# Two of four channel groups of a 31-tap depthwise convolution, as products with diagonal matrices on TensorE

## The chip, the cores and the metric

The kernel runs as one program on one core of a Trainium2 chip. The metric is the device time of one execution in microseconds (us); a lower time is better. Engines are named as in the profile: PE is TensorE, DVE is VectorE, ACT is ScalarE, POOL is GpSimd, SP issues most DMAs.

## The reference

Two transformer-like blocks run one after the other on 512 rows of width 1024. The first has a mixer with two branches (a gated convolution and a latent attention) and a feed-forward part; the second has sparse attention, a recurrent branch and a mixture of experts. The change touches only the convolution branch of the first block:

```
def conformer_conv(u, dw_w, dw_b, ln_g, ln_b):
    a, gte = jnp.split(u, 2, axis=-1)
    v = a * jax.nn.sigmoid(gte)
    v = dwconv(v, dw_w, dw_b)          # 31 taps, one filter per channel, 512 channels
    return jax.nn.silu(layer_norm(v, ln_g, ln_b))
```

Beside it, from the same normalised input, the attention branch computes latent rows `cq` and `ckv` (products with `w_in`), an RMS norm of each row, and from these queries, keys and values.

## The kernel before, in words

All of it is in `block1`. Channels lie on partitions, so the 512 channels are four groups of 128. Products are made in three parts with fp32r operands: `split` writes a high part on ACT and the rest on DVE, and `mm3` (lines 85 to 87) issues three matmuls, high by high, low by high, high by low.

The work around the change stands in this order in the code.

1. **Gate stage.** For each group `c`, two products `lin` of 24 matmuls of 512 columns give the gate and the value; ACT takes the sigmoid (line 464) and DVE writes `vpad[:, c]` (line 467), the gated rows with 15 zeros on either side. Between them go steps of `mods`: each loads 1 MB of `w_ada` and issues four fp32 matmuls (line 286).
2. **Latent stage.** Ten products `lat`, six of 288 columns (keys and values) and four of 384 (queries), 24 matmuls each. After each, `rms_rows` squares the row on ACT (line 518), DVE and POOL make the inverse root (lines 123 and 124, `ss`), DVE scales the row (line 520, `cn`). One product later PE transposes `cn` (line 541). Key rows also get a rotation on DVE (lines 508 to 511) and POOL (lines 512 and 513, `krow`). After each product come one or two steps of `mods` and `go(conv, 4)`.
3. **Expansion stage.** Products of the latent rows with `w_ukv` (512 columns, into `dbank`) and `w_uq` (384 columns), again with `go(conv, ...)`, and then the attention proper, whose first PE work is the transposes of line 655.

The convolution itself is the generator `taps`, which `go(conv, n)` advances. Groups 0 to 2 are on DVE: one `scalar_tensor_tensor` per tap (line 486), 93 with the first ones. Group 3 is on POOL: a product (line 479) and a sum (line 481) per tap. The sums `cacc` are first read by `conv_norm` (line 630), inside the attention.

The order of instructions on each engine is not that of the code: a scheduler sets it from its own estimate of times, engine by engine, and each engine then runs its list in order. A pool `psd` holds two PSUM tiles `dbank`; `mods` holds one of them until it ends. The out-projection behind the attention ends in a layer norm of four row tiles `xr` (lines 779 to 786), whose transposed, split rows `hh` and `hl` (lines 163 and 164) feed the feed-forward part.

Of the kernel before, what the change touches and what calls it, by code (L numbers as in the profile page):

```python
# [9 lines left out]
F32 = mybir.dt.float32  # L10
F32R = mybir.dt.float32r
# [3 lines left out]
AF = mybir.ActivationFunctionType  # L15
ALU = mybir.AluOpType
# [4 lines left out]
S = 512  # L21
# [39 lines left out]
class Kernel:  # L61
# [203 lines left out]
    def close(self, *cms):  # L265
        for cm in cms:
            cm.__exit__(None, None, None)
# [70 lines left out]
    def block1(self):  # L338
        tc, nc, io = self.tc, self.nc, self.io
        v, act, pe, pool_e = nc.vector, nc.scalar, nc.tensor, nc.gpsimd  # L340
        op, close = self.open, self.close
# [7 lines left out]
        pC_cm, pC = op("pC", side="left")  # L349
# [3 lines left out]
        pA_cm, pA = op("pA", side="right")  # L353
# [28 lines left out]
        vpad = pV.tile([128, 4, S + 30], F32, name="vpad")  # L382
        cacc = pV.tile([128, 4, S], F32, name="cacc")
# [12 lines left out]
        _, mt = self.mod_turn(md[:, 0:512], pLw)  # L396
# [13 lines left out]
        col = self.col  # L410
# [12 lines left out]
        pM_cm = pM = None  # L423
# [24 lines left out]
        go = lambda gen, n: [None for _ in range(n) if next(gen, 0) == 0]  # L448
# [4 lines left out]
        for c in range(4):  # L453
# [13 lines left out]
            v.tensor_tensor(vpad[:, c, 15:S + 15], psa, sg, op=ALU.mult)  # L467
            go(mods, 1 if c >= 0 else 0)

        def taps():  # L470
            cw = col["conv_dw_w"]
            todo = [[(c, i) for c in range(3) for i in range(31)], [(3, i) for i in range(31)]]
            while todo[0]:
                for eng, lst, n in ((v, todo[0], 3), (pool_e, todo[1], 1)):
                    for _ in range(n):
                        c, i = lst.pop(0)
                        if eng is pool_e and i:
                            w = pC.tile([128, S], F32, name="tap")
                            eng.tensor_scalar(w, vpad[:, c, i:i + S], cw[:, i * 4 + c:i * 4 + c + 1], 1.0,
                                              op0=ALU.mult, op1=ALU.mult)  # L480
                            eng.tensor_tensor(cacc[:, c, :], cacc[:, c, :], w, op=ALU.add)
                        elif i == 0:
                            eng.tensor_scalar(cacc[:, c, :], vpad[:, c, 0:S], cw[:, c:c + 1], col["conv_dw_b"][:, c:c + 1],
                                              op0=ALU.mult, op1=ALU.add)
                        else:
                            eng.scalar_tensor_tensor(cacc[:, c, :], vpad[:, c, i:i + S], cw[:, i * 4 + c:i * 4 + c + 1],  # L486
                                                     cacc[:, c, :], op0=ALU.mult, op1=ALU.add)
                        yield
        conv = taps()


# [10 lines left out]
        def rope(dst, src, t, nh):  # L502

            cs = self.rope[:, t, 0:16].unsqueeze(1).to_broadcast([128, nh, 16])
            sn = self.rope[:, t, 16:32].unsqueeze(1).to_broadcast([128, nh, 16])
            a, b = src[:, :, 0:16], src[:, :, 16:32]
            w = pLw.tile([128, 8, 32], F32, name="ropew")
            v.tensor_tensor(w[:, :nh, 0:16], b, sn, op=ALU.mult)
            v.tensor_tensor(w[:, :nh, 16:32], a, sn, op=ALU.mult)
            v.tensor_tensor(dst[:, :, 0:16], a, cs, op=ALU.mult)  # L510
            v.tensor_tensor(dst[:, :, 16:32], b, cs, op=ALU.mult)
            pool_e.tensor_tensor(dst[:, :, 0:16], dst[:, :, 0:16], w[:, :nh, 0:16], op=ALU.subtract)
            pool_e.tensor_tensor(dst[:, :, 16:32], dst[:, :, 16:32], w[:, :nh, 16:32], op=ALU.add)
# [11 lines left out]
        def lat(t, wts, n):  # L525
            a, b, sl = (hch, hcl, slice(t * 128, (t + 1) * 128)) if t < 2 else (h1h, h1l, slice((t - 2) * 128, (t - 1) * 128))
            ps = self.bank()
            for k in range(8):
                wh, wl = wts[k // 4]
                self.mm3(ps[:, :n], (a[:, k, sl], b[:, k, sl]), (wh[:, k % 4, :], wl[:, k % 4, :]), k == 0, k == 7)  # L530
            return ps

        def latent(ps, t, n, g, hi, lo):
            cn = pLw.tile([128, 384], F32, name="cn")
            rms_rows(cn[:, :n], ps[:, 0:n], n, g)
            return cn, t, n, hi, lo
# [10 lines left out]
        def flush(n=0):  # L547
            while len(pend) > n:
                turn_latent(*pend.pop(0))

        for t in range(6):
            ps = lat(t, wk, 288)
            if t < 2:
                act.activation(krow[:, t, :], ps[:, 256:288], AF.Copy)
            else:
                rope(krow[:, t:t + 1, :], ps[:, 256:288].unsqueeze(1), t - 2, 1)
            pend.append(latent(ps, t, 256, kg, ckh, ckl))
            flush(1)
            go(mods, 1)
            go(conv, 4)  # L560
        wq = [self.wblock(w_in, 4 * h, 4, 1024, 384) for h in range(2)]
        for t in range(NT):
            pend.append(latent(lat(t + 2, wq, 384), t, 384, qg, cqh, cql))
            flush(1)
            go(mods, 2)
            go(conv, 4)
        flush()
        go(mods, 99)
        close(pM_cm, pA_cm)
        pQ_cm, pQ = op("pQ", side="right")  # L570
        k96 = pQ.tile([128, 6, 8, 96], F32, name="k96")
        q96 = pQ.tile([128, NT, 8, 96], F32, name="q96")
# [2 lines left out]
        for t in range(6):  # L575
            pool_e.tensor_scalar(k96[:, t, :, 64:96], krow[:, t:t + 1, :].to_broadcast([128, 8, 32]), 1.0, 1.0,
                                 op0=ALU.mult, op1=ALU.mult)
# [129 lines left out]
        for i in range(len(items)):  # L707
            h, t = items[i]
# [35 lines left out]
        for n in range(2):  # L744
            c = slice(n * 512, (n + 1) * 512)
# [22 lines left out]
        for t in range(NT):  # L768
# [5 lines left out]
            for n in range(2):  # L774
                c = slice(n * 512, (n + 1) * 512)
# [4 lines left out]
            s, b, _ = self.ln_stats([xr[:, 0:512], xr[:, 512:1024]], LN_EPS)  # L780
# [17 lines left out]
        pM_cm, pM = op("pM2", 2, side="right")  # L798
# [71 lines left out]
        hh, hl = self.hh, self.hl  # L870
# [23 lines left out]
        for t in range(NT):  # L894
            sl = slice(t * 128, (t + 1) * 128)
            y = ys[t]
            for k in range(18, 22):
                down(ks, ws, t, k)
            for n in range(2):
                c = slice(n * 512, (n + 1) * 512)  # L900
# [1453 lines left out]
```

## Time and profile before

| | us |
|---|---|
| median of 3 runs | 2093.3 |
| lowest and highest of them | 2086.33 and 2097.59 |
| profiled execution, its own time | 2086.47 |
| its span in the trace | 2084.7 |
| PE busy | 1918.0 (92%) |
| DVE busy | 1175.3 (56%) |
| ACT busy | 661.3 (32%) |
| POOL busy | 555.2 (27%) |

The span is what the trace shows; the profiled execution's own time has 1.8 us around it. Busy shares are means over a program of many stages; the change lies in the first ninth of it, so what it is worth is read from the rows of that part.

### The profile page before, as it was taken

What the parts mean: (1) busy time and instruction counts of PE and PEld (TensorE: products, weight loads), DVE (VectorE), ACT (ScalarE), POOL (GpSimd) and SP (SyncE); (2) the same over time, 40 slices, a digit from 0 to 9 for tenths busy, and PEclk for the clock granted to TensorE, in tenths of its full rate; (3) what the DMA queues carried; (4) which work ended last, traced back from release to release, by engine and by line L of the source; (5) the groups of instructions that cost most, each with busy time, mean ns of one, the idle gap of its engine ahead of it and who ended that gap; (6) DMA issues with size and microseconds to landing.
All of it is one profiled execution on the core that took longest, in us unless ns stands there. A gap on an engine that the chain in (4) does not pass through costs nothing.

```text
span 2084.7 us, 30137 instructions
## 1 busy us (share of the span) xinstructions
PE 1918.0 (92%) x11420; PEld 1461.2 (70%) x11427; DVE 1175.3 (56%) x2137; ACT 661.3 (32%) x1168; POOL 555.2 (27%) x448
## 2 busy tenths in 40 slices
PE   4978898979999998997899999999899999999993
PEld 2657786777777887875677877788676666767662
DVE  4896576588574468565897576667332332222223
ACT  3213466434333325544323245523111111111111
POOL 1279422352012432012002100143122322223222
PEclk8989899989999999999799999999899999999997
DMA  8651102378462223549767631553999999999895
GB/s 284 215 185 60 51 1 78 110 253 296 141 208 97 101 91 115 153 127 236 223 177 177 170 114 62 172 166 133 358 327 360 306 381 329 354 362 336 316 367 173
DMA packets 208751, 425.47 MB, mean 204 GB/s; under 512 B 46694, under 2 KB 140280, under 8 KB 182485
## 3 DMA queue, kind: packets, MB, share of 16 engines
q1 hardware_dynamic: 184914, 366.98, 50.6%
q0 software_dynamic: 15488, 39.41, 7.7%
q10 hardware_dynamic: 8195, 17.06, 2.2%
q8 instruction: 92, 1.51, 0.3%
q14 instruction: 62, 0.51, 0.1%
HBM read 375.37 MB, written 60.08 MB: 209 GB/s over the span
## 4 chain that ended last, share of the span: by engine, by line
PE 70%; DVE 10%; DMA 7%; issue 5%; ACT 3%; POOL 3%; SPq 1%; POOLq 0%; ACTq 0%; DVEq 0%
PE bank L85 10%; PE bank L87 10%; PE bank L86 10%; PE gbank L2146 9%; PE wbank L2201 6%; PE bank L2132 3%; PE bank L2109 2%; PE gbank L2157 2%; PE dbank L85 2%; PE dbank L87 2%; PE dbank L86 2%; DVE cacc L486 1%; DMA ysum_db<-y,idxr 1%; DVE wlo L81 1%; PE wbank L2190 1%
## 5 line engine op out<-in xcount | busy, mean ns | idle before, releaser
L81 DVE TENSOR_TENSOR wlo<-raw,whi 128x1024 fp32r<-128x1024 f32 (+2 forms) x163 | 221.0, 1376 | 111.5 <-ACT whi L80 107.6
L85 PE MATMUL bank<-hh,whi 128*128 128x512 f32 (+3 forms) x720 | 273.2, 383 | 3.5 <-DVE hh L163 3.0
L86 PE MATMUL bank<-hl,whi 128*128 128x512 f32 (+3 forms) x720 | 273.4, 381 | 1.5 <-DVE hl L164 1.5
L87 PE MATMUL bank<-hh,wlo 128*128 128x512 f32 (+3 forms) x720 | 273.1, 382 | 1.0 <-DVE wlo L81 1.0
L80 ACT ACTIVATE whi<-raw 128x1024 fp32r<-128x1024 f32 (+2 forms) x163 | 161.7, 1025 | 241.9 <-PE bank L86 175.9
L2146 PE MATMUL gbank<-wr,xt 128*128 128x256 f32 x928 | 210.5, 385 | 0.9 <-issue 0.3
L2146 PEld LDWEIGHTS gbank<-wr,xt 128*128 128x128 f32 x928 | 175.7, 192 | 24.9 <-ACT xt L2115 1.0
L87 PEld LDWEIGHTS bank<-hh,wlo 128*128 128x128 f32 (+2 forms) x720 | 137.0, 191 | 35.3 <-issue 3.9
L85 PEld LDWEIGHTS bank<-hh,whi 128*128 128x128 f32 (+2 forms) x720 | 137.2, 192 | 32.1 <-DVE hh L163 3.4
L86 PEld LDWEIGHTS bank<-hl,whi 128*128 128x128 f32 (+2 forms) x720 | 137.7, 191 | 29.3 <-DVE hl L164 2.3
L2201 PE MATMUL wbank<-wr,ht 128*128 128x512 f32 (+2 forms) x456 | 138.7, 599 | 6.6 <-ACT ht L2173 5.6
L2162 DVE TENSOR_TENSOR h<-gbank,h 128x256 f32<-128x256 f32 (+1 forms) x40 | 17.0, 426 | 217.0 <-ACT h L2161 217.0
L2183 DVE SCALAR_TENSOR_TENSOR y<-wbank,wt,g2l 128x512 f32<-128x512 f32 (+1 forms) x69 | 51.7, 750 | 129.6 <-PE wbank L2201 110.3
L2201 PEld LDWEIGHTS wbank<-wr,ht 128*128 128x128 f32 (+2 forms) x456 | 51.2, 154 | 73.1 <-issue 62.8
L866 POOL TENSOR_TENSOR hid<-ug,uv 128x512 f32<-128x512 f32 x22 | 36.1, 1643 | 181.3 <-DVE uv L850 181.3
L486 DVE SCALAR_TENSOR_TENSOR cacc<-vpad,cols,cacc 128x512 f32<-128x512 f32 x90 | 83.6, 968 | 0.4
L2161 ACT ACTIVATE h<-gbank 128x256 f32<-128x256 f32 (+1 forms) x40 | 15.2, 381 | 210.8 <-PE gbank L2146 174.8
L2098 POOL DMA_INDIRECT xg<-h_d,idx x40 | 41.1, 1028 | 129.8 <-DVE idx L2093 80.2
L621 POOL TENSOR_TENSOR raw<-raw,g2row 128x2048 f32<-128x2048 f32 x11 | 55.0, 4999 | 73.8 <-DMA raw<-in_w_down_dram 73.5
L2132 PE MATMUL bank<-wr,xt 128*32 128x256 f32 (+1 forms) x896 | 65.9, 381 | 0.7 <-ACT xt L2115 0.2
L1990 POOL DMA_INDIRECT ysum_da<-y,idx x21 | 32.8, 1560 | 118.6 <-DVE y L2183 86.1
L2109 PEld LDWEIGHTS bank<-ident,xg 128*128 128x128 f32 (+1 forms) x392 | 48.8, 195 | 20.3 <-issue 15.3
(692 smaller groups left out, 4263.5 us busy)
## 6 DMA issues: line engine op xcount, KB each, us to landing
wr<-in_exp_gate_dram SPq DMA_DIRECT2D x52, 1024.0 KB
wr<-in_exp_up_dram SPq DMA_DIRECT2D x52, 1024.0 KB
wr<-in_exp_down_dram SPq DMA_DIRECT2D x52, 1024.0 KB
raw<-in_w_in_dram SPq DMA_DIRECT2D x58, 512.0 KB
mraw<-in_w_ada_dram SPq DMA_DIRECT2D x24, 1024.0 KB
mraw<-in_ada_w_dram SPq DMA_DIRECT2D x24, 1024.0 KB
raw<-in_w_up_dram SPq DMA_DIRECT2D x22, 1024.0 KB
raw<-in_w_down_dram SPq DMA_DIRECT2D x11, 1024.0 KB
```

The source lines that it names most:

```text
L80: self.nc.scalar.activation(hi, src, AF.Copy)
L81: self.nc.vector.tensor_tensor(lo, src, hi.bitcast(F32), op=ALU.subtract)
L85: mm(out, a[0], b[0], start=start, stop=False, skip_group_check=True)
L86: mm(out, a[0], b[1], start=False, stop=False, skip_group_check=True)
L87: mm(out, a[1], b[0], start=False, stop=stop, skip_group_check=True)
L486: eng.scalar_tensor_tensor(cacc[:, c, :], vpad[:, c, i:i + S], cw[:, i * 4 + c:i * 4 + c + 1], cacc[:, c, :], op0=ALU.mult, op1=ALU.add)
L621: return lambda raw, k, n: pool_e.tensor_tensor(raw, raw, row.unsqueeze(1).to_broadcast([128, k, n]), op=ALU.mult)
L2109: pe.transpose(ps[:, k * 128:k * 128 + r], x.rearrange("s (p k) -> s k p", k=8)[0:r, 4 * g + k, :], self.ident[0:r, 0:r])
L2132: pe.matmul(ps[to, 0:256], job.xt[:, k, sl], x[:, k * 256:(k + 1) * 256], start=k == 0, stop=k == 7, skip_group_check=True)
L2146: pe.matmul(ps[:, m * 256:(m + 1) * 256], job.xt[:, k, :], w[m][:, k * 256:(k + 1) * 256], start=k == 0, stop=k == 7, skip_group_check=True)
L2183: end = lambda c, ps: v.scalar_tensor_tensor(y[r, c], ps, job.wt[r], g2row[r, c], op0=ALU.mult, op1=ALU.mult)
L2201: pe.matmul(ps[to], job.ht[:, k, sl], x[:, k * D + c.start:k * D + c.stop], start=k == 0, stop=k == 1, skip_group_check=True)
```

## The change

Groups 0 and 1 of the convolution leave DVE. For each of their 62 taps ACT makes two diagonal matrices of 128 x 128, the identity scaled per partition by the high and the low part of that tap's weights; `mm3` then adds diagonal times shifted rows to `cps`, a `dbank` that holds both groups. The rows `vpad` of the two groups and the weights are split once. At the end of a group ACT copies the sum to `cacc` and adds the bias. Group 2 stays on DVE and group 3 on POOL, so `taps` now yields 62 times instead of 124. `go(conv_pe, 6)` and `go(conv_pe, 7)` stand in the latent stage, and `go(conv_pe, 99)` at its end.

```
--- before.py
+++ after.py
@@ -467,25 +467,44 @@
             v.tensor_tensor(vpad[:, c, 15:S + 15], psa, sg, op=ALU.mult)
             go(mods, 1 if c >= 0 else 0)
 
+
+        pD_cm, pD = op("pD", side="right")
+        wc = [pD.tile([128, 62], F32R, name="wc" + x) for x in "hl"]
+        cw = col["conv_dw_w"].rearrange("p (i c) -> p i c", c=4)[:, :, 0:2]
+        two = lambda t: t.rearrange("p (i c) -> p i c", c=2)
+        self.split(two(wc[0]), two(wc[1]), cw)
+        vs = [pD.tile([128, 2, S + 30], F32R, name="vs" + x) for x in "hl"]
+        for c in range(2):
+            self.split(vs[0][:, c, :], vs[1][:, c, :], vpad[:, c, :])
+        cps = self.dbank()
+
+        def diagonal_taps():
+            for c in range(2):
+                for i in range(31):
+                    d = [pD.tile([128, 128], F32R, name="diag" + x, bufs=8) for x in "hl"]
+                    for x, y in zip(d, wc):
+                        act.activation(x, self.ident, AF.Copy, scale=y.bitcast(F32)[:, 2 * i + c:2 * i + c + 1])
+                    self.mm3(cps[:, c * 512:(c + 1) * 512], d, [x[:, c, i:i + S] for x in vs], i == 0, i == 30)
+                    yield
+                act.activation(cacc[:, c, :], cps[:, c * 512:(c + 1) * 512], AF.Identity, bias=col["conv_dw_b"][:, c:c + 1], scale=1.0)
+
         def taps():
             cw = col["conv_dw_w"]
-            todo = [[(c, i) for c in range(3) for i in range(31)], [(3, i) for i in range(31)]]
-            while todo[0]:
-                for eng, lst, n in ((v, todo[0], 3), (pool_e, todo[1], 1)):
-                    for _ in range(n):
-                        c, i = lst.pop(0)
-                        if eng is pool_e and i:
-                            w = pC.tile([128, S], F32, name="tap")
-                            eng.tensor_scalar(w, vpad[:, c, i:i + S], cw[:, i * 4 + c:i * 4 + c + 1], 1.0,
-                                              op0=ALU.mult, op1=ALU.mult)
-                            eng.tensor_tensor(cacc[:, c, :], cacc[:, c, :], w, op=ALU.add)
-                        elif i == 0:
-                            eng.tensor_scalar(cacc[:, c, :], vpad[:, c, 0:S], cw[:, c:c + 1], col["conv_dw_b"][:, c:c + 1],
-                                              op0=ALU.mult, op1=ALU.add)
-                        else:
-                            eng.scalar_tensor_tensor(cacc[:, c, :], vpad[:, c, i:i + S], cw[:, i * 4 + c:i * 4 + c + 1],
-                                                     cacc[:, c, :], op0=ALU.mult, op1=ALU.add)
-                        yield
+            for i in range(31):
+                for c, eng in ((2, v), (3, pool_e)):
+                    if eng is pool_e and i:
+                        w = pC.tile([128, S], F32, name="tap")
+                        eng.tensor_scalar(w, vpad[:, c, i:i + S], cw[:, i * 4 + c:i * 4 + c + 1], 1.0,
+                                          op0=ALU.mult, op1=ALU.mult)
+                        eng.tensor_tensor(cacc[:, c, :], cacc[:, c, :], w, op=ALU.add)
+                    elif i == 0:
+                        eng.tensor_scalar(cacc[:, c, :], vpad[:, c, 0:S], cw[:, c:c + 1], col["conv_dw_b"][:, c:c + 1],
+                                          op0=ALU.mult, op1=ALU.add)
+                    else:
+                        eng.scalar_tensor_tensor(cacc[:, c, :], vpad[:, c, i:i + S], cw[:, i * 4 + c:i * 4 + c + 1],
+                                                 cacc[:, c, :], op0=ALU.mult, op1=ALU.add)
+                    yield
+        conv_pe = diagonal_taps()
         conv = taps()
 
 
@@ -557,16 +576,19 @@
             pend.append(latent(ps, t, 256, kg, ckh, ckl))
             flush(1)
             go(mods, 1)
+            go(conv_pe, 6)
             go(conv, 4)
         wq = [self.wblock(w_in, 4 * h, 4, 1024, 384) for h in range(2)]
         for t in range(NT):
             pend.append(latent(lat(t + 2, wq, 384), t, 384, qg, cqh, cql))
             flush(1)
             go(mods, 2)
+            go(conv_pe, 7)
             go(conv, 4)
         flush()
         go(mods, 99)
-        close(pM_cm, pA_cm)
+        go(conv_pe, 99)
+        close(pD_cm, pM_cm, pA_cm)
         pQ_cm, pQ = op("pQ", side="right")
         k96 = pQ.tile([128, 6, 8, 96], F32, name="k96")
         q96 = pQ.tile([128, NT, 8, 96], F32, name="q96")
```

The order on the engines, before and after, at the places that the prediction speaks of. First PE in the latent stage, between the product of one key row tile and the next. In these rows `whi,h1h` is a latent product, `mraw,scp` a step of `mods`, `ident,cn` the transposes of the row tile before. Of the kernel before:

```order
L87 MATMUL bank<-whi,h1l 128x288
L286 MATMUL dbank<-mraw_1174,scp 32x512 x4
L541 MATMUL bank<-ident,cn 128x128 x2
L85 MATMUL bank<-whi,h1h 128x288
```

And of the changed kernel, where `vsh,diagh` is a tap's product; six taps stand here, of which the first and the last are shown:

```order
L87 MATMUL bank<-whi,h1l 128x288
L560 MATMUL bank<-ident,cn 128x128 x2
L286 MATMUL dbank<-mraw_1043,scp 32x512 x4
L85 MATMUL dbank<-vsh,diagh 128x512
L86 MATMUL dbank<-vsl,diagh 128x512
L87 MATMUL dbank<-vsh,diagl 128x512
...
L85 MATMUL dbank<-vsh,diagh 128x512
L86 MATMUL dbank<-vsl,diagh 128x512
L87 MATMUL dbank<-vsh,diagl 128x512
L85 MATMUL bank<-whi,h1h 128x288
```

Eighteen matmuls of taps now stand between the step of `mods` and the next product; all 186 stand before the first product of the expansion stage, one of them in the gate stage.

Then DVE in the latent stage, around two row tiles. Of the kernel before:

```order
L508 TENSOR_TENSOR ropew<-bank,rope 128x16
L509 TENSOR_TENSOR ropew<-bank,rope 128x16
L510 TENSOR_TENSOR krow<-bank,rope 128x16
L511 TENSOR_TENSOR krow<-bank,rope 128x16
L486 SCALAR_TENSOR_TENSOR cacc<-vpad,cols_337,cacc 128x512
L520 SCALAR_TENSOR_TENSOR cn<-bank,ss,kg 128x256
L486 SCALAR_TENSOR_TENSOR cacc<-vpad,cols_337,cacc 128x512
L123 TENSOR_SCALAR ss<-ss 128x1
L486 SCALAR_TENSOR_TENSOR cacc<-vpad,cols_337,cacc 128x512 x2
L141 TENSOR_TENSOR ckl<-bank,ckh 128x2x128
```

And of the changed kernel, from its last taps on:

```order
L539 SCALAR_TENSOR_TENSOR cn<-bank,ss,kg 128x256
L504 SCALAR_TENSOR_TENSOR cacc<-vpad,cols_337,cacc 128x512 x4
L527 TENSOR_TENSOR ropew<-bank,rope 128x16
L528 TENSOR_TENSOR ropew<-bank,rope 128x16
L529 TENSOR_TENSOR krow<-bank,rope 128x16
L530 TENSOR_TENSOR krow<-bank,rope 128x16
L141 TENSOR_TENSOR ckl<-bank,ckh 128x2x128
L123 TENSOR_SCALAR ss<-ss 128x1
L539 SCALAR_TENSOR_TENSOR cn<-bank,ss,kg 128x256
```

Taps stood between all of DVE's steps of the latent rows; now the 31 that are left end at the third row tile, and behind it no tap stands on DVE.

Last, DVE at the end of the out-projection, where the statistics of the last row tile (`mv`, lines 123, 132, 134), the splits of the next weights (`wlo`) and the splits of turned rows (`hh`, `hl`) meet. Of the kernel before:

```order
L779 TENSOR_TENSOR xr<-xr,dbank 128x512
L164 TENSOR_TENSOR hl<-turned,hh 128x4x128
L134 SCALAR_TENSOR_TENSOR mv<-mv 128x1
L130 BN_STATS bnst<-xr 128x6
L81 TENSOR_TENSOR wlo<-raw,whi 128x1024 x2
L132 BN_AGGR mv<-bnst 128x2
L81 TENSOR_TENSOR wlo<-raw,whi 128x1024 x2
L123 TENSOR_SCALAR mv<-mv 128x1
L134 SCALAR_TENSOR_TENSOR mv<-mv 128x1
L163 CAST hh<-turned 128x4x128
```

And of the changed kernel:

```order
L801 TENSOR_TENSOR xr<-xr,dbank 128x512
L163 CAST hh<-turned 128x4x128
L130 BN_STATS bnst<-xr 128x6
L164 TENSOR_TENSOR hl<-turned,hh 128x4x128
L163 CAST hh<-turned 128x4x128
L132 BN_AGGR mv<-bnst 128x2
L81 TENSOR_TENSOR wlo<-raw,whi 128x1024
L164 TENSOR_TENSOR hl<-turned,hh 128x4x128
L123 TENSOR_SCALAR mv<-mv 128x1
L81 TENSOR_TENSOR wlo<-raw,whi 128x1024
L134 SCALAR_TENSOR_TENSOR mv<-mv 128x1
L81 TENSOR_TENSOR wlo<-raw,whi 128x1024 x2
```

The last tile's line 123 stood behind four splits of weights and now stands behind one.

## Rows read from the trace of the kernel before

**Rows 1.** Windows: stretch, length, busy of each engine, granted clock, DMA share, GB/s.
```profile
core 0: us, PE busy (x) PEld busy (x) DVE busy (x) ACT busy (x) POOL busy (x), PEclk, DMA share, GB/s
66.20:110.14 43.94, 43.94 (x199) 29.09 (x199) 39.12 (x55) 6.99 (x10) 0.00 (x0) 0.94 0.82 279
110.14:188.60 78.46, 60.96 (x358) 48.45 (x357) 70.92 (x103) 15.19 (x38) 71.21 (x63) 0.87 0.39 140
188.60:226.44 37.84, 33.21 (x151) 29.21 (x149) 15.10 (x44) 12.94 (x27) 24.26 (x37) 0.91 0.06 16
426.35:446.00 19.65, 9.12 (x44) 7.95 (x43) 18.84 (x10) 5.12 (x14) 15.58 (x7) 0.58 0.22 79
```

**Rows 2.** The page's costliest groups: DVE's taps (count, busy us, mean ns).
```profile
L486 DVE SCALAR_TENSOR_TENSOR cacc<-vpad,cols,cacc 128x512 f32<-128x512 f32 x90 | 83.6, 968 | 0.4
```

**Rows 3.** Waits of PE, 110.14 to 188.60: total us, times, longest.
```profile
PE bank L541 <- DVE cn L520: 11.2, 3, 5.3
PE dbank L286 <- DMA mraw<-in_w_ada_dram: 6.0, 2, 4.2
```

**Rows 4.** Waits of PE, 188.60 to 226.44.
```profile
PE bank L541 <- DVE cn L520: 2.5, 1, 2.5
PE bank L85 <- ACT whi L80: 2.1, 1, 2.1
```

**Rows 5.** PE timeline, gate stage: start us, length, engine, line, operation.
```profile
95.65 1.07 PE L286 MATMUL dbank<-mraw,scp 128*32 128x512 f32 x8
96.65 0.50 PE L86 MATMUL bank<-h1l,whi 128*128 128x512 f32 x1
96.99 0.40 PE L87 MATMUL bank<-h1h,wlo 128*128 128x512 f32 x1
97.22 0.40 PE L85 MATMUL bank<-h1h,whi 128*128 128x512 f32 x1
```

**Rows 6.** PE timeline, a latent product of 288 and one of 384 columns, first and next.
```profile
136.57 0.38 PE L85 MATMUL bank<-whi,h1h 128*128 128x288 f32 x1
...
139.92 0.64 PE L286 MATMUL dbank<-mraw,scp 128*32 128x512 f32 x4
...
179.47 0.42 PE L85 MATMUL bank<-whi,h1h 128*128 128x384 f32 x1
...
183.79 0.38 PE L541 MATMUL bank<-ident,cn 128*128 128x128 f32 x2
```

**Rows 7.** PE timeline, the products behind the wait for `cn` in the expansion stage.
```profile
197.90 0.52 PE L85 MATMUL bank<-whi,cqh 128*128 128x384 f32 x1
198.22 0.52 PE L86 MATMUL bank<-wlo,cqh 128*128 128x384 f32 x1
```

**Rows 8.** POOL timeline, taps early and late.
```profile
119.20 1.01 POOL L479 TENSOR_SCALAR tap<-vpad,cols 128x512 f32<-128x512 f32 x1
...
122.00 1.01 POOL L479 TENSOR_SCALAR tap<-vpad,cols 128x512 f32<-128x512 f32 x1
...
205.16 0.69 POOL L479 TENSOR_SCALAR tap<-vpad,cols 128x512 f32<-128x512 f32 x1
...
207.33 0.69 POOL L479 TENSOR_SCALAR tap<-vpad,cols 128x512 f32<-128x512 f32 x1
```

**Rows 9.** ACT timeline, tiles of 128 x 124 and 128 x 128.
```profile
46.25 0.91 ACT L257 ACTIVATE cols<-bank 128x124 f32<-128x124 f32 x4 [0.47 <-PE bank L256]
...
407.85 5.90 ACT L160 ACTIVATE turned<-bank,fb,fs 128x128 f32<-128x128 f32 x16 [1.06 <-PE bank L156]
```

**Rows 10.** ACT and DVE timelines, end of the out-projection.
```profile
424.33 1.24 ACT L781 ACTIVATE xr<-xr,mv 128x1024 f32<-128x1024 f32 x1 [4.62 <-DVE mv L134]
...
418.93 2.31 DVE L81 TENSOR_TENSOR wlo<-raw,whi 128x1024 fp32r<-128x1024 f32 x2
421.15 0.15 DVE L123 TENSOR_SCALAR mv<-mv 128x1 f32<-128x1 f32 x1
```

## The prediction

> **What bounds the kernel now.** I read the stretches first, then the costliest groups, then PE's waits in the two stretches where PE is not always busy, and then the timelines around the places that the change touches.
>
> In the gate stage, 66.2 to 110.14, PE is busy for the whole of 43.94 us [rows 1]. DVE is busy for 39.12 of them, much of it taps, and PE waits for none of it. What DVE sheds there is worth nothing.
>
> In the latent stage, 110.14 to 188.60, PE is busy for 60.96 of 78.46 us at a granted clock of 0.87, DVE for 70.92 and POOL for 71.21 [rows 1]. PE waits 11.2 us for `cn` in three long waits, and 6.0 us for a DMA of `w_ada` rows [rows 3]. This stage is not bounded by PE; it has holes, and the taps of PE are put into them. So the first question is how much room there is.
>
> In the expansion stage, 188.60 to 226.44, PE is busy for 33.21 of 37.84 us [rows 1]. It waits once for the last `cn` (2.5) and once for a weight split on ACT (2.1) [rows 4].
>
> DVE's 93 taps cost 0.968 us each [rows 2]. No one of them stands on the path by itself; they matter where DVE's `cn` stands behind them. That is the 11.2 and the 2.5.
>
> **The change: PE in the latent stage.** It adds 62 taps of three matmuls of 512 columns, 186 in all, one of which goes to the gate stage. The trace of before has this very form in the gate stage: an fp32r matmul of 512 columns with its own weights starts 0.2333 us after the one before (96.99 to 97.22) [rows 5]. 185 x 0.2333 = 43.2 us at the full clock.
>
> The work that PE has in this stage without taps, at the full clock, is made of:
> - six products of 288 columns, 3.35 each (136.57 to 139.92): 20.1
> - four of 384 columns, 4.32 each (179.47 to 183.79) [rows 6]: 17.3, and with 0.1 less where no clock ramp is in it 16.8
> - nine steps of `mods` at 1.0 (95.65 to 96.65, eight records of four matmuls) [rows 5]: 9.0, and 1.6 for the changes of kind between them, just under 0.2 each
> - transposes and small products of the modulation rows: about 5.3, estimated from their counts
>
> With 19.2 for the first term (3.2 each, again without what the ramp adds) that is 51.9. The taps make it 95.1. I take 1.5 us for waits for `cn` that remain, so 96.6 against 78.46 before: **+18.1**. The room in the stage was thus some 25 us (waits and half clock), and 43 are put in.
>
> Why only 1.5 of waits. DVE loses 62 taps, 60.0 us [rows 2]; of the 31 that are left the last stand at the third row tile, so from then on `cn` stands behind no tap on DVE. But each `cn` also needs POOL's inverse root, and POOL keeps its 31 taps. A pair of POOL instructions takes 2.80 us early, while DVE runs taps (119.20 to 122.00), and 2.17 late, when DVE runs few (205.16 to 207.33) [rows 8]. With DVE's taps gone by the third row tile I take 2.17 for most of them. POOL then has 6 to 8.6 us of taps per row tile, and PE a step of about 8.9 us (a product, one `mods`, six taps): balanced, POOL a little ahead. Bounds: no wait at all, +16.6; pairs that stay at 2.80, some 20 to 30 taps times 0.63 later, 12 to 19 us of which PE meets most: +30.
>
> The diagonals are new work of ACT: 124 tiles of 128 x 128. The nearest rows are a copy of 128 x 124, 0.91/4 = 0.23 us, and one of 128 x 128 with scale and bias per partition, 5.90/16 = 0.37 us [rows 9]. That is 29 to 46 us on an engine that is busy for 15.19 of 78.46 there [rows 1]. A step of six taps wants twelve of them, 2.7 to 4.4 us, while PE needs 8.9 for it. Eight buffers of each part let ACT run eight taps ahead. Price 0; the cover is PE's own step. Were ACT to run late, because a diagonal stands behind a square of a row that PE has not made, a tap would wait; the longest price is a whole step's 4.4 us once in each of ten steps, which I do not expect. The two splits of `vpad` and of the weights are a handful of passes over 542 columns, in the gate stage, where ACT is busy for 6.99 of 43.94 us.
>
> A tap's rows start at every offset of 4 bytes; no row shows an fp32r matmul that reads rows off a round address. I price this at nothing, since DVE and POOL read the same offsets here at one price per tap, and give the other case a rival.
>
> The Trainium skill ("TensorE: Matmul & The Clock Gate", section "Back-to-back issue gap") says that a stream of weight loads and matmuls of 512 columns sustains about 131 ns for each, less than the 216 ns it gives for one alone. By that the 185 matmuls would be 24.2 us (an estimate from that page), and the sum about 19 less. The gate stage is such a stream, and its row says 233 ns [rows 5]; the row decides.
>
> **Expansion stage.** PE's transposes of the last `cn` stood after 2.5 us of waiting, and behind it the products ran at half clock: 0.32 from one start to the next (197.90 to 198.22) [rows 7], against 4.32/24 = 0.18 at the full clock [rows 6]. Nine of them did so: 9 x 0.14 = 1.3. In the changed order taps and a product of `w_ukv` stand ahead of these transposes, so the wait is covered and the clock does not fall: 37.84 - 2.5 - 1.3 = 34.0, of which I give 0.2 back. **-3.6.** The wait of 2.1 for `whi` stays, because both weight buffers are in use until the product ahead ends. Bounds: 0, if the new wait is as long; -5.9, if that wait is gone too (2.1 more).
>
> **Attention.** The orders of PE, ACT and DVE there are the old ones but for names. `cacc` is read late in it, long after any engine's last tap. 0.
>
> **The end of the out-projection, 426.35 to 446.00.** The scheduler has moved four weight splits on DVE. In this stretch PE is busy for only 9.12 of 19.65 us, at a clock of 0.58 [rows 1], because the last row tile's layer norm is awaited. Its line 123 ran at 421.15, behind two pairs of splits, of which the last took 2.31 us, 1.16 each; ACT's scaling of that row, which waited 4.62 us for it, began at 424.33 [rows 10]. Now one split stands ahead in place of four: 3 x 1.16 = 3.5 us, of which I take **-3**, as some of that moves into the casts that stand ahead now. Bounds: +3 (those casts wait for ACT's turned rows); -14, if PE's holes there (19.65 - 9.12 = 10.5) and what the clock costs (9.12 x 0.42 = 3.8) close altogether.
>
> **The rest.** The feed-forward part behind it has PE busy throughout, in the same work; behind that the orders are equal. 0.
>
> **Sum.** +18.1 - 3.6 - 3 = +11.5 on the profiled execution's 2086.5: 2098.0. That execution was at the low end of the three runs; their median is 2093.3, 6.8 higher. Against the median the sum would be 2104.8. I give **2101**, half way between the two.
>
> **The rivals.** About 0.5% (10.4 us) is what a measurement of this kernel can tell from no change.
>
> 1. *POOL or ACT feed PE too slowly* (22%). POOL's chain paces `cn` before (11.2 us of waits [rows 3]) and keeps all its taps; if its pairs stay at 2.80 [rows 8], or diagonals stand behind a square, PE waits 7 to 15 us more: +17 to +33, some 2112. For it: POOL was busy for 71.21 of 78.46 us [rows 1]. Against: DVE's share of the conflict goes.
>
> 2. *The far waits close altogether* (21%): no wait in the latent stage (+16.6), 5.9 won in the expansion stage, and the end of the out-projection gains up to 14: 16.6 - 5.9 - 14 = -3, to +7 where it gains 4; about 2090. It speaks for this that the last stretch has a PE at 0.58 clock [rows 1]; against it, that the three other row tiles' chains there remain.
>
> 3. *Faster than before, by cheaper matmuls* (5%). PE's price for a column differs between the forms: 3.35/24 = 0.140 us for 288 columns, 0.49 ns a column, against 0.456 in the gate stage [rows 5, 6]; if a tap's matmul, whose price no row shows with a diagonal as weights, took no more than the 0.140 of the shorter product, then 185 x 0.140 = 25.9, 17.3 less, and the whole comes to -6, 2081 to 2087. It decides from below 0.17 us a matmul on. Against it stands the row of the same form.
>
> 4. *Taps cost more* (5%): offsets that slow the reading, or a clock that falls in the stage because PE waits for each diagonal. At the half clock's 0.32 x 512/384 = 0.43 us [rows 7], 185 x 0.43 = 79.6: +36 and more on the sum, 2135 to 2140.
>
> The forecast has 47%: +7 to +17 on either base.
>
> **How the numbers follow.** Slower by over 0.5%: about half of the forecast's cases (.24), all of rival 1 but its lowest end, rival 4 and little of rival 2: .24 + .22 + .05 + .02 = .53. Faster by over 0.5%: the end of rival 2 and rival 3: .08. Within: .39. The range, 2087 to 2117, leaves out rival 3, rival 4, the upper end of rival 1 and the lower of rival 2, some 2 in 10.
>
> **What would show it.** In the changed kernel: a latent stage of 95 to 98 us with PE busy for nearly all of it at a clock near 1.0; tap matmuls 0.233 us apart, first to next; waits for `cn` of 0 to 2 us; an expansion stage of 34; POOL's pairs near 2.2 after the third row tile; no waits of PE for a diagonal beyond the first; the last layer norm 3 us earlier; attention and feed-forward stretches of the old lengths. I am wrong on the room if PE waits for POOL's chain or for diagonals, wrong on the price if the matmuls lie closer or further apart, and wrong on the remainder if a stretch behind 226 us changes by more than 1 us other than at the end of the out-projection.

## The result, and the profile after

The changed kernel takes 2115.66 us (median of 6 runs, 2106.59 to 2130.45) against 2092.4 (6 runs, 2086.33 to 2099.14): a ratio of 1.0115, 95% interval 1.0087 to 1.0144, which is 18 to 30 us slower. The sum of the prediction, against the median, was 11.5 slower. The profiled execution took 2118.48 us, 32.0 more than that of before. The range held it, near its upper end, and the sign was right, but it lies above the +7 to +17 of the likeliest case. So there are two questions: does the forecast 11.5 stand in the trace, and what is the rest?

Busy time on the page of the changed kernel, share of the span and instructions:

```profile
PE 1971.5 (93%) x11613; PEld 1503.6 (71%) x11613; DVE 1133.8 (54%) x2078; ACT 704.8 (33%) x1297; POOL 545.5 (26%) x448
```

PE has 53.5 us more (1971.5 against 1918.0), DVE 42 less, ACT 44 more, the diagonals. The windows of the changed kernel, in the columns of [rows 1]: end of the gate stage, latent stage, expansion stage.

```profile
66.00:108.18 42.18, 42.18 (x202) 26.81 (x201) 17.71 (x23) 10.14 (x18) 0.03 (x1) 0.98 0.85 284
108.18:205.78 97.60, 94.75 (x539) 75.57 (x535) 44.39 (x78) 52.66 (x151) 79.45 (x83) 1.00 0.31 106
205.78:237.70 31.92, 29.80 (x148) 26.16 (x147) 10.82 (x39) 11.31 (x23) 5.00 (x17) 1.00 0.04 16
```

Read against [rows 1], from the second row on: the latent stage is 97.6 us long in place of 78.5, PE is busy for 94.75 of it, and the clock is 1.00 in place of 0.87. DVE falls from 70.9 to 44.4 us, and nothing is won by that alone. The expansion stage is 31.9 long in place of 37.8. The first row is not the same work as that of [rows 1], since the changed kernel stood 3 us further on at 66 us; the latent stage starts at 108.18 in place of 110.14. Of PE's waits in both stages, this is all that is left:

```profile
PE bank L85 <- ACT whi L80: 2.1, 1, 2.1
PE bank L560 <- DVE ss L123: 1.5, 1, 1.5
PE bank L560 <- DVE cn L539: 1.3, 2, 1.2
```

PE has no wait for a diagonal in it. The taps themselves, on PE's timeline of the changed kernel:

```profile
131.68 0.50 PE L85 MATMUL dbank<-vsh,diagh 128*128 128x512 f32 x1
132.01 0.39 PE L86 MATMUL dbank<-vsl,diagh 128*128 128x512 f32 x1
132.24 0.39 PE L87 MATMUL dbank<-vsh,diagl 128*128 128x512 f32 x1
132.47 0.40 PE L85 MATMUL dbank<-vsh,diagh 128*128 128x512 f32 x1
132.71 0.40 PE L86 MATMUL dbank<-vsl,diagh 128*128 128x512 f32 x1
...
135.95 0.29 PE L85 MATMUL bank<-whi,h1h 128*128 128x288 f32 x1
```

From 132.01 on they start 0.23 us apart, as in [rows 5]; the first after another kind of product takes 0.1 more. Eighteen of them, with the first one's 0.1, fill 131.68 to 135.95, 0.237 each.

The attention begins at 237.70 in place of 226.44, 11.3 later. It stays near there for long: what stood at 939 and 1108 us in before is 13 and 15 late. Then, in the second block's recurrent branch, where PE's instructions and their order are the old ones, another 18 are lost: what stood at 1262 us is 33.6 late. The clock shows it; windows of the changed kernel there:

```profile
1180.00:1186.00 6.00, 5.97 (x118) 5.68 (x116) 5.39 (x9) 2.50 (x5) 0.00 (x0) 1.00 0.63 156
1186.00:1192.00 6.00, 6.00 (x56) 5.66 (x57) 1.38 (x2) 0.00 (x0) 0.00 (x0) 0.61 0.42 147
1192.00:1198.00 6.00, 6.00 (x70) 5.77 (x67) 2.06 (x3) 1.18 (x2) 0.00 (x0) 0.50 0.09 26
1222.00:1252.00 30.00, 30.00 (x132) 21.74 (x131) 15.81 (x42) 11.72 (x31) 0.00 (x0) 0.50 0.40 110
```

The granted clock is 0.5 there, the 1.2 GHz level. PE is busy all through these windows, as far as the modelled ends of its matmuls tell. Ahead of the first fall, at some 1188 us, stand products of 64 x 64, and from 1180 on no gap over 0.03 us; ahead of the second, at 1222, stands one wait of 0.56 us for a DMA, at 1216. In the profile of before the same matmuls ran at 1.00. Whether the change does this was the first thing to find out.

### The profile page after: what moved, and what is told of

Its sections match the earlier page's. It is cut to its first block, busy times and chain, and to the rows that moved or that the text cites. A ratio compares the mean times of both kernels' runs of the same rounds, so it can differ in the third digit from the quotient of the medians.

```text
span 2116.7 us, 30617 instructions
## 1 busy us (share of the span) xinstructions
PE 1971.5 (93%) x11613; PEld 1503.6 (71%) x11613; DVE 1133.8 (54%) x2078; ACT 704.8 (33%) x1297; POOL 545.5 (26%) x448
## 4 chain that ended last, share of the span: by engine, by line
PE 71%; DVE 8%; DMA 8%; issue 5%; POOL 4%; ACT 3%; SPq 1%; ACTq 0%; POOLq 0%; DVEq 0%
PE bank L85 10%; PE bank L86 10%; PE bank L87 10%; PE gbank L2168 9%; PE wbank L2223 6%; PE bank L2154 3%; PE dbank L85 2%; PE dbank L87 2%; PE dbank L86 2%; PE bank L2131 2%; PE gbank L2179 2%; DVE wlo L81 1%; POOL cacc L499 1%; DMA ysum_db<-y,idxr 1%; DMA mraw<-in_w_ada_dram 1%
## 5 line engine op out<-in xcount | busy, mean ns | idle before, releaser
L2137 ACT ACTIVATE xt<-bank 128x512 f32<-128x512 f32 (+1 forms) x49 | 26.9, 549 | 95.1 <-PE bank L2131 63.1
```

## The experiments

### 1. Both kernels again

No edit. **Expected** of before:

> The kernel of before, unchanged, with a second profile. In the first pair of profiles the changed kernel is 11.3 us late where the attention begins, 12.4 at the feed-forward part, 15 before the recurrent branch, and 33 behind it, where the same matmuls in the same order ran at a granted clock of 0.5 for two stretches of some 13 and 31 us. Theory A (those low stretches fall by accident, in executions of either kernel): the stretch from 1160 to 1290 shows low-clock pieces here too in some executions, in other places than before, and the times spread by 10 us or more. Theory B (the change brings them about): the stretch is the old one within 1 us, clock near 1.0, and the times spread by less.

and of the changed kernel:

> The changed kernel, unchanged, with a second profile. Theory A (accident): the attention begins 11.3 +-1 us later than before again, and the recurrent branch has low-clock stretches of another length and place, or none: an execution without them takes some 2100. Theory B (the change causes the fall of the clock): the two stretches at 0.5 are there again in the same places and cost 17 us within 3.

**Measured.** Before again: 2100.55 us (10 runs, 2090.38 to 2106.11); that is 1.0024 times the runs of before measured beside it (median 2094.31), 0.9999 to 1.0049. The changed kernel: 2112.18 (9 runs, 2100.24 to 2121.22), 1.0082, 1.0049 to 1.0114. The second profile of before has the low clock in the recurrent branch too:

```profile
1192.00:1222.00 30.00, 28.81 (x127) 20.84 (x127) 15.06 (x38) 11.21 (x30) 0.00 (x0) 0.53 0.43 126
1222.00:1240.00 18.00, 18.00 (x114) 13.99 (x113) 10.91 (x30) 6.68 (x18) 0.00 (x0) 0.69 0.26 82
```

The second one of the changed kernel has hardly any: of 25 windows of 5 us from 1165 on, 24 are at 1.00. So theory A holds: the clock falls in either kernel, and the ten times of before lie 15.7 us apart. In the ten profiles told of here and below, the low pieces in that stretch of the branch differ from one execution to the next, from one or two pieces of under 4 us to 30 us and more.

Four profiles now give the change without that branch. From the views of single lines of PE, three marks in each: the attention's first transposes, a first product `iwT` in the second block, and the first transposes behind the recurrent branch; count, shortest, median and longest ns, first and last start. Before:

```profile
L655 PE MATMUL bank<-ident,q x32: 270/272/286, 226.4 to 319.7; 128*96 128x128 f32 x32
...
L1133 PE MATMUL bank<-ident,iwT x4: 208/208/229, 938.9 to 939.1; 16*128 16x16 f32 x4
...
L1715 PE MATMUL qbank<-ident,h x16: 272/360/476, 1423.5 to 1430.0; 128*128 128x128 f32 x16
```

Before again:

```profile
L655 PE MATMUL bank<-ident,q x32: 270/272/286, 222.9 to 316.2; 128*96 128x128 f32 x32
...
L1133 PE MATMUL bank<-ident,iwT x4: 207/208/229, 935.1 to 935.3; 16*128 16x16 f32 x4
...
L1715 PE MATMUL qbank<-ident,h x16: 272/360/476, 1437.4 to 1443.9; 128*128 128x128 f32 x16
```

The changed kernel:

```profile
L677 PE MATMUL bank<-ident,q x32: 270/272/286, 237.7 to 332.5; 128*96 128x128 f32 x32
...
L1155 PE MATMUL bank<-ident,iwT x4: 208/208/230, 951.9 to 952.1; 16*128 16x16 f32 x4
...
L1737 PE MATMUL qbank<-ident,h x16: 270/347/473, 1457.1 to 1462.7; 128*128 128x128 f32 x16
```

The changed kernel again:

```profile
L677 PE MATMUL bank<-ident,q x32: 270/272/286, 239.9 to 332.9; 128*96 128x128 f32 x32
...
L1155 PE MATMUL bank<-ident,iwT x4: 208/208/231, 954.7 to 954.9; 16*128 16x16 f32 x4
...
L1737 PE MATMUL qbank<-ident,h x16: 270/347/474, 1443.1 to 1449.3; 128*128 128x128 f32 x16
```

The differences of these marks, and of the spans (2084.7, 2097.9, 2116.7, 2102.4):

| stretch | before | before again | changed | changed again | change of the means |
|---|---|---|---|---|---|
| start to the attention | 226.4 | 222.9 | 237.7 | 239.9 | +14.2 |
| from there to the mark `iwT` | 712.5 | 712.2 | 714.2 | 714.8 | +2.2 |
| over the recurrent branch | 484.6 | 502.3 | 505.2 | 488.4 | by the clock, no sign |
| from there to the end of the span | 661.2 | 660.5 | 659.6 | 659.3 | -1.4 |

One part of the expectation failed: the attention of the changed kernel begins 17.0 later in the second pair, not 11.3 within 1. The 5.7 between the pairs lie mostly in two places. The latent stage starts at 110.14 and 107.31 us in before and at 108.18 and 108.74 in the changed kernel, 2.0 earlier in the first pair and 1.4 later in the second. And the expansion stage of the changed kernel takes 31.9 and 33.5 us. The latent stage itself differs by at most 0.6 between two profiles of one kernel. So one pair of profiles does not tell this change to better than some 3 us.

Without the third row the change is 14.2 + 2.2 - 1.4 = 15.0 us slower. The third row spreads by 17 to 18 us within either kernel. Of the two profiles with the least low clock, the spans are 2084.7 and 2102.4, 17.7 apart.

### 2. VectorE's relief without TensorE's load

```
-        conv_pe = diagonal_taps()
+        v.memset(cacc[:, 0:2, :], 0.0)
+        conv_pe = iter(())
```

> The two groups are left out altogether: no taps for them on any engine (their part of the convolution is zero); the splits of vpad stay. It prices the relief of VectorE apart from the load on TensorE. Room theory: TensorE's work is 44 us less than in the changed kernel, and the holes that come back are the DMA of w_ada (6.0 us) and POOL's chain (some 3 to 8): the attention begins at 237.7 - 44 + 9 to 14 = 203 to 208, 18 to 23 us earlier than before. Rival (POOL's taps pace cn, so that VectorE's relief is worth little): the attention begins at 215 or later.

**Measured.** The first transposes of the attention:

```profile
L678 PE MATMUL bank<-ident,q x32: 270/272/285, 204.9 to 297.7; 128*96 128x128 f32 x32
```

The attention begins at 204.9, within what was expected: 19.7 earlier than before (224.65, the mean of two). PE still waits 8.2 us for `cn` and `ss`, 5.5 of them in the latent stage and 2.7 in the expansion stage, against 11.2 + 2.5 in before [rows 3, 4]. The 6.0 us of DMA that were expected back did not come. So the relief is worth 20 us there, and the 186 matmuls on PE cost 238.8 - 204.9 = 33.9 of their 44. The total, 2188.86 us, is not a price: the values behind the convolution are others. From the third mark to the end of the span it takes 776.7 us in place of 659.6, and one group of the mixture of experts' matmuls has 992 of them in place of 928.

### 3. One group in place of two

```
-        for c in range(2):
+        for c in range(1):
...
-                for c, eng in ((2, v), (3, pool_e)):
+                for c, eng in ((1, v), (2, v), (3, pool_e)):
...
-            go(conv_pe, 6)
+            go(conv_pe, 3)
...
-            go(conv_pe, 7)
+            go(conv_pe, 4)
```

The first line stands for the loop of the splits and for that of the taps.

> One group alone on TensorE (93 matmuls), two on VectorE, one on GpSimd; TensorE takes three or four taps after each row tile in place of six or seven. Room theory (the change costs what does not fit into TensorE's holes): 93 x 0.237 = 22.0 us less TensorE work than in the changed kernel, so the attention begins at 237.7 - 22.0 = 215.7 plus 3 to 7 us of waits for cn that come back: 219 to 223 against 226.4 before, total 3 to 7 us below before. Rival (VectorE's taps still pace cn, since 62 of 93 stay): waits for cn of 9 us or more, attention at 226 or later, total as before or above it.

**Measured.** 2098.84 us, 1.0011 (0.9987 to 1.0035): as before. The attention begins at 228.7, not at 219 to 223; this expectation of mine was wrong:

```profile
L677 PE MATMUL bank<-ident,q x32: 270/272/286, 228.7 to 321.6; 128*96 128x128 f32 x32
```

PE waits 8.2 us for `cn` and `ss`, 6.1 in the latent stage and 2.1 in the expansion stage, and of these waits one has the low clock behind it (144 to 148 us). Of the 22 us taken off PE, 10 show at that mark. The rival foretold the mark and the total; its 9 us of waits were not quite reached. But the rival's reason, that DVE's taps hold `cn`, does not follow yet: each `cn` also needs an inverse root from POOL.

### 4. One matmul per tap

```
-                    self.mm3(cps[:, c * 512:(c + 1) * 512], d, [x[:, c, i:i + S] for x in vs], i == 0, i == 30)
+                    self.nc.tensor.matmul(cps[:, c * 512:(c + 1) * 512], d[0], vs[0][:, c, i:i + S], start=i == 0, stop=i == 30, skip_group_check=True)
```

> The changed kernel with one matmul per tap, high by high; the two products with low parts are left out, the diagonals of the low parts stay. 124 matmuls fewer, 29.4 us at 0.237. If the stage stays bounded by TensorE, the attention begins at 238.8 - 29.4 = 209.4; if the waits for cn come back as in the version without the two groups (8.2 us), at 215 to 218. If the changed kernel's stage was bounded by the diagonals on ACT rather than by matmuls, the attention begins at 230 or later.

**Measured.** 2092.76 us, 0.9987 (0.9959 to 1.0014). The attention begins at 216.2, with 6.9 us of waits for `cn`: the second case.

```profile
L677 PE MATMUL bank<-ident,q x32: 270/272/287, 216.2 to 311.3; 128*96 128x128 f32 x32
```

ACT made as many diagonals as before and held nothing up; PE's matmuls were the bound of the changed kernel, and as soon as they are fewer, `cn` is late again, with only 31 taps on DVE. That pointed at POOL.

### 5. GpSimd's taps behind its last inverse root

In the three kernels (before, changed, one group), the taps of group 3 become a generator of their own, with an order edge (`late[0]`) to the last inverse root of the latent stage, and are advanced in the expansion stage and the attention:

```
+        def late_taps():
+            for i in range(31):
+                with tc.issue_after(late[0]):
...
+                        pool_e.tensor_scalar(w, vpad[:, 3, i:i + S], cw[:, i * 4 + 3:i * 4 + 4], 1.0, op0=ALU.mult, op1=ALU.mult)
+                        pool_e.tensor_tensor(cacc[:, 3, :], cacc[:, 3, :], w, op=ALU.add)
```

> The kernel of before with one edit: GpSimd's group of taps stands behind its last inverse root of the latent stage, and runs beside the expansion stage and the attention. VectorE keeps three groups. POOL theory (the tap pairs on POOL, not the taps on VectorE, hold back cn): the 11 to 14 us of waits for cn and the half clock behind them go, the 6 us of DMA stay; the attention begins at 198 to 206 against 222.9 and 226.4, and the total is 18 to 25 us below before, unless POOL's taps delay the attention's P. VectorE theory (93 taps there hold cn): waits for cn of 8 us or more stay, and the attention begins at 216 or later.

> The changed kernel with the same edit. Both theories see a TensorE that is busy throughout the latent stage, so only the 2.8 us of waits for cn and ss can go: the attention begins at 235 to 238 (237.7 and 239.9 in the changed kernel), the total is 1 to 4 us below the changed kernel and still 13 or more above before.

> One group on TensorE, two on VectorE, and GpSimd's group behind its last inverse root. POOL theory: the waits for cn of the version with one group (7.0 + 1.2 in the latent stage, 2.1 ahead of the expansion, and the half clock behind them) go, and the stage is bounded by TensorE: the attention begins at 213 to 218, 10 to 15 us earlier than there (228.7). VectorE theory: 225 or later.

**Measured.**

| | attention begins | with the edit | time with the edit | ratio to before, interval |
|---|---|---|---|---|
| before | 226.4, 222.9 | 200.9 | 2069.01 | 0.9867, 0.9823 to 0.9911 |
| one group | 228.7 | 215.9 | 2089.69 | 0.9964, 0.9929 to 0.9999 |
| changed | 237.7, 239.9 | 236.0 | 2099.69 | 1.0036, 1.0003 to 1.0070 |

The starts with the edit, in the order of the table:

```profile
L672 PE MATMUL bank<-ident,q x32: 270/272/314, 200.9 to 293.8; 128*96 128x128 f32 x32
L694 PE MATMUL bank<-ident,q x32: 270/272/314, 215.9 to 311.6; 128*96 128x128 f32 x32
L694 PE MATMUL bank<-ident,q x32: 270/272/314, 236.0 to 330.0; 128*96 128x128 f32 x32
```

All three starts of the attention fall where the POOL theory put them. The changed kernel's total fell by more than the 1 to 4 us expected: it is 12.5 below the 2112.18 of experiment 1, and 5.0 above before in place of the 13 or more expected. Its profile shows 5.2 of this by the marks of experiment 1: 2.8 at the start of the attention, against the mean of the two profiles, 1.6 from there to `iwT` and 0.8 at the end. Over the recurrent branch it takes 487.9 us, as the cleaner of the two did (488.4), and 7 of its 10 runs lie between 2097.29 and 2100.01. So the rest fits fewer low pieces there, which was not shown for the runs without a profile.

In before with the edit, with all 93 taps still on DVE, these are all of PE's waits in the latent stage:

```profile
PE dbank L286 <- DMA mraw<-in_w_ada_dram: 2.3, 4, 0.8
PE bank L300 <- ACT modr L297: 0.4, 1, 0.4
```

where the expectation kept 6 us of DMA, and these the windows of its latent and expansion stage:

```profile
110.08:167.38 57.30, 54.56 (x358) 41.19 (x357) 48.73 (x103) 14.88 (x38) 13.45 (x17) 1.00 0.52 190
167.38:200.90 33.52, 30.12 (x151) 26.12 (x149) 13.87 (x40) 12.85 (x27) 31.78 (x41) 1.00 0.06 18
```

57.3 us where before took 78.5, the clock at 1.00, and no matmul put on PE or taken off. This edit alone beats both kernels, by 25.7 us on the median of before measured beside it (2094.74), in four runs, with an interval of 18.6 to 37.1. It does not keep all that it wins at the attention's start, 23.8 us: from there to the mark `iwT` it takes 718.0 in place of 712.4, with POOL's taps now beside the attention, and the end takes 0.7 more. So 17.5 us stand outside the recurrent branch; what the other 8 of the medians are was not shown. The profiled run is the slowest of the four, and takes 494.0 over that branch, as before does in the mean (493.5), so fewer low pieces in the other three would do it.

What POOL's taps did is seen in two ways. The first is the queue of POOL. In before's latent stage PE's transposes waited 5.30 us for a `cn`:

```profile
147.15 0.66 PE L541 MATMUL bank<-ident,cn 128*128 128x128 f32 x2 [5.30 <-DVE cn L520]
```

The POOL timeline ahead of that one, and DVE's:

```profile
143.09 0.66 POOL L513 TENSOR_TENSOR krow<-krow,ropew 128x16 f32<-128x16 f32 x1
143.74 1.80 POOL L479 TENSOR_SCALAR tap<-vpad,cols 128x512 f32<-128x512 f32 x1
145.51 0.97 POOL L124 TENSOR_TENSOR ss<-ss,mhalf 128x1 f32<-128x1 f32 x1
```

```profile
142.09 1.59 DVE L486 SCALAR_TENSOR_TENSOR cacc<-vpad,cols,cacc 128x512 f32<-128x512 f32 x1
143.60 0.14 DVE L123 TENSOR_SCALAR ss<-ss 128x1 f32<-128x1 f32 x1
```

DVE had the input of that inverse root done at 143.74. The root ran from 145.51, behind a tap of 1.80, and took 0.97 for 128 numbers; in the mean it takes 0.84 in before's latent stage and 0.65 in the changed kernel's. DVE's list has its share too: ACT's sum of the row was done at 141.74, and line 123 stood until 143.60, the last 1.5 us of it behind a tap of DVE. Ahead of the transposes of 172.06, for which PE waited 4.65 us, both stand again: the row's sum was done at 162.46, line 123 ran at 167.52 behind splits and taps on DVE, and the root at 170.94 behind taps on POOL, with DVE idle for 2.46 us until it was done.

The second way is that DVE's own taps are slower beside POOL's. The group of DVE's taps in the latent stage, before, and before with the edit, count, busy, mean ns:

```profile
L486 DVE SCALAR_TENSOR_TENSOR cacc<-vpad,cols,cacc 128x512 f32<-128x512 f32 x48 | 54.2, 1161 | 0.1
```

```profile
L486 DVE SCALAR_TENSOR_TENSOR cacc<-vpad,cols,cacc 128x512 f32<-128x512 f32 x48 | 34.1, 747 | 0.1
```

The same 48 taps take 20.1 us less. How much of the gain comes from POOL's queue and how much from the faster taps was not tried apart. Experiment 2, with 31 taps on DVE, has both in its 8.2 us of waits. In 2.7 of them no tap is left on DVE, and the root begins 5.5 us after line 123, behind POOL's work. Ahead of the longest wait, 3.65, it was POOL that sat idle for 0.22 until line 123 came, behind DVE's taps of 1.2 us and more.

## Why the prediction was right, and where it was not

**The latent stage: right.** 97.60 and 97.63 us in the two profiles, against 96.6 forecast; matmuls at 0.233 to 0.237, clock 1.00, waits of 2.8 us in place of the 1.5 taken. (The two starts that [rows 5] shows give 0.23; the 0.2333 of the prediction is what was measured.) Against 78.46 and 77.83 before this is +19.1 and +19.8 for the term +18.1. Diagonals at 0.40 us were a little above the bound from [rows 9] and hidden, as costed at nothing. That experiment 4 took 124 matmuls off and won 22.6 us at the attention's start, with all diagonals still made, shows that PE was the bound.

**The expansion stage: right in its mechanism.** 31.92 and 33.53 us against 37.84 and 37.76 before: -5.9 and -4.2 in place of -3.6. The wait for `whi` stayed, as said. The pairs differ in what the clock did behind it: the 63 products there took 12.9 us in both profiles of before and in the second one of the changed kernel (226.98 to 239.90), and 11.3 in the first (226.38 to 237.70). So those 1.6 us are not the change's, and without them the term is -4.3 and -4.2.

With the start of the latent stage, 2.0 earlier in one pair and 1.4 later in the other, the attention came 11.3 and 17.0 late, 14.2 in the mean; the terms +18.1 and -3.6 make 14.5. That this agrees so well is in part luck: in the mean the latent stage cost 1.4 more than forecast, and the expansion stage won 1.5 more, half of it by the low clock.

**What held `cn`: half of it, without harm to the sum.** The prediction put the 11.2 and 2.5 us of [rows 3, 4] down to `cn` standing behind DVE's taps, with POOL as a second limit. Experiment 5 closed these waits with as many of DVE's taps left in the latent stage as before, 48. So DVE's taps alone do not make them: the late `cn` came through both lists, one behind the other, and POOL's taps made DVE's longer. Rival 1 says of the kernel of before that POOL's chain paces `cn`, which is nearer to what was found. The relief of DVE did win 20 us (experiment 2), in part through POOL, whose tap pairs went from 2.80 to 2.17 as foretold from [rows 8]. The sum counted only that PE would be without holes, whoever had made them, so it came out.

**The end of the out-projection: the step that failed, -3 forecast, -0.4 found.** From the attention's start to the first feed-forward product behind the turned rows: 211.3 and 211.2 in before (437.71 and 434.06), 210.7 and 211.0 in the changed one (448.40 and 450.91). The first half of the step came true. DVE and POOL of the changed kernel:

```profile
429.07 0.15 DVE L123 TENSOR_SCALAR mv<-mv 128x1 f32<-128x1 f32 x1
...
430.54 2.35 DVE L134 SCALAR_TENSOR_TENSOR mv<-mv 128x1 f32<-128x1 f32 x1
432.82 4.54 DVE L81 TENSOR_TENSOR wlo<-raw,whi 128x1024 fp32r<-128x1024 f32 x2
437.28 2.61 DVE L163 CAST hh<-turned 128x512 fp32r<-128x512 f32 x1
```

```profile
429.81 6.46 POOL L807 TENSOR_TENSOR xr<-xr,lg 128x1024 f32<-128x1024 f32 x2
```

Line 123 was at 421.15 [rows 10]; with the 11.3 of the later start it would be 432.4, so it came 3.3 early. But the splits of `wlo` that it overtook now stand behind it, where POOL scales `xr`, and there two of them take 4.54 us, where two took 2.31 [rows 10]. The first cast starts at 437.28; before it was 426.99, with the 11.3 438.25. Of 3.3 us one is left, and 0.4 of it goes in the casts and splits of turned rows that follow, up to 2.7 us each beside POOL: from that first cast to the product it takes 11.1 us, in before 10.7. The second pair shows the same, with 4.53 for the two splits: line 123 came 5.1 early, the first cast 2.7, the product 0.2. So the steps behind the first cast lose up to 2.5. No edit tested this step. The prediction moved work off the path without asking what it would run beside.

**The feed-forward part: 0 forecast, some +2.5 found.** Waits of the changed kernel between 457 and 952 that before does not have: 1.3 for `kl`, 1.2 for `ug`, 0.7 more for `wlo`. They sum to 3.2, less 0.7 that a wait for `iwT` lost; the second pair shows the same ones, and 0.7 for `uv`. DVE's steps and splits stand in another order there than in before, which the prediction took as the same work; that this order makes the waits is likely, but was not tested. By its own sign, a stretch behind 226 us that changes by more than 1 us, the prediction was wrong on the remainder. What the -1.4 at the end comes from was not looked into.

**The base.** The prediction took the sum on one profiled execution that had run nearly without the low clock in the recurrent branch, and gave half of the distance to the median back. Both kernels' medians hold some of it. The permanent part of the change is 15.0 by the table and 17.7 by the two cleanest profiles; the medians, measured twice, gave 23.3 and 17.9. Of the 32.0 us between the first two profiles 20.6 lie in the third row of that table, the rows of low clock. That the first of these lies above the permanent part for the same reason is likely but was not shown: what decides when the clock falls was not found, nor whether the changed kernel has it more often. So the range held the 23.3 in part by luck: its upper end was there for rival 1, which has PE wait 7 to 15 us more for POOL or ACT, and PE waits 2.8 us in all.

## What to carry to other kernels

Before moving work off an engine that stands ahead of a wait, ask who else the late result needs: here a result of one number per row crossed DVE and POOL, and putting POOL's bulk work behind it won 25.7 us by the medians and 17.5 by the marks, with nothing moved to PE, where two groups on PE lost some 15 by the marks. An engine with holes is a poor place for more work than the holes hold: with POOL's taps out of the way, PE's 44 us of taps cost 35.1 (200.9 to 236.0). And take two profiles of each kernel before reading a difference of 1%: a stretch with nothing changed spread by 17 to 18 us here.

## What the runs showed of the hardware

TensorE's granted clock fell from 1.00 to 0.50, the 1.2 GHz level, at some 1188 us of the changed kernel, in a stretch of products of 64 x 64, with PE busy for 5.97 of the 6 us from 1180 on and for all of the next 6. It fell again at 1222, for 30 us of mixed products, with one wait of 0.56 us at 1216 ahead of it. In the second profile of the same program the first fall did not come, and the second was a piece of under 4 us. The Trainium skill ("TensorE: Matmul & The Clock Gate", section "What's actually happening") gives an idle stretch as what brings the low level on; the rows of the first fall show it without one, as far as the modelled ends of the matmuls tell.

A tap of 128 x 512 on DVE took 0.75 us without POOL's taps and 1.16 beside them, POOL's pair 2.17 and 2.80. The Trainium skill ("SBUF — State Buffer", section "Who interferes with whom") says that a DVE instruction with two SBUF inputs contends with a GpSimd one that reads SBUF. The taps are such instructions, and the trace agrees. Whoever adds up the busy times of both as if they ran free prices a plan too low.
